# Mixture of experts on one core: one compact iteration per expert, and fp32 products without splits for experts of at most 64 tokens

## The chip, the cores and the metric

The kernel runs on one core of a Trainium2 chip. The metric is the device time of one execution in microseconds (us). The kernel before was timed three times; the median counts.

## The reference

One decoder block for 512 tokens of width 1024. The first half (state-space mixer, pooling mixer, gates) is not touched by the change. The second half sends every token to 8 of 64 experts:

```python
_, top_e = lax.top_k(masked, TOP_K)                # 512 tokens x 8 experts
def expert_block(args):                            # 128 slots of one expert
    toks, ws, e = args
    xb = u_pad[toks]
    hid = jax.nn.silu(xb @ we_gate[e]) * (xb @ we_up[e])    # 1024 -> 256, twice
    return (hid @ we_down[e]) * ws[:, None]                 # 256 -> 1024
```

All is float32. Each expert has three weights of 1 MB (gate, up, down). The routing of these inputs is uneven: 34 experts have at most 64 tokens (two of them none; expert 0, with 49, is one of the 34), 19 have 65 to 128, and 11 have 132 to 165. In the order 0 to 63, with l for at most 64, h for 65 to 128, H for more and 0 for none:

```
lhHHllHlHllHhl0hlhllHHlhHllhHlHlhhhhllllhhlll0hhlllhhllHhhlllllh
```

## The kernel before

TensorE (PE) multiplies fp32 numbers as three fp32r products. `split` (lines 43 to 46) makes a high part on ACT (a cast) and a low part on DVE (a subtraction), and `mm3` (lines 58 to 62) issues high by high, low by high and high by low. Both operands are split: the tokens (`turn`: gathered rows are transposed on PE, 8 transposes of 128x128, and evacuated as `xh` and `xl`) and the weights (`Unit.split`: 128x2048 from a raw tile into `h` and `l`, three of them per expert).

`experts` holds the 64 experts as straight-line code, one iteration for each, with the instructions written out by hand (`manual_schedule`). Tokens sit in blocks of 128 slots: a block of an expert is gathered from DRAM by GpSimd (`gather`, an indirect DMA into `xg`), multiplied, weighted and added to the output rows by another indirect DMA (`scatter`). An expert of more than 128 tokens has a second block. The text says single for an iteration of one block and double for one of two.

In iteration e of a single, PE multiplies gate and up of expert e (`gate_up_mm`, 8 slices of the contraction, 24 instructions of 512 columns), transposes the tokens of e+1, multiplies down of e-1 (`down`, 12 instructions of 512 columns), transposes the hidden rows of e (`down_in`), and makes the slot list of e+4 (`index`, tile `ixp`). Beside it ACT and DVE split gate and up of e+1 and down of e. One branch at the head of the iteration chooses between the code for one block, for none and for two:

```python
with tc.If(n_e <= P) as big:            # line 1113
    with tc.If(n_e > 0) as some:        # line 1114
        ...
with big.Else():
    turn(k, k.xg[3 + e % 2], xnext)
```

SP loads the weights (`load(e + 2)` in iteration e; a load is skipped for an expert without tokens) into eight raw tiles of 1 MB that are used in turn, so a tile is written again eight units, or 2.67 experts, later. It is free once the split that reads it is done. GpSimd's queue holds the gathers and scatters, each within conditionals by the number of rows; line 1065 is the conditional of the second block.

Of the kernel before, what the change touches and what calls it, by code (L numbers as in the profile page):

```python
# [21 lines left out]
P = 128  # L22
T = 512
NT = 4
D = 1024
NK = 8
H = 32
G = 8
E = 64
NC = 8  # L30
# [814 lines left out]

def slot_onehot(k, pm, nb, eng):

    oh = k.wp.tile([P, NT, nb, P], BF16, name="oh", bufs=2)
    for t in range(NT):
        eng.tensor_scalar(oh[:, t], k.iota[:, :nb, :], pm[:, t:t + 1], None, op0=ALU.is_equal)  # L850
    return oh
# [21 lines left out]
    return xg  # L873


def turn(k, src, x, full=None):

    nc = k.nc
    xv = src.rearrange("p (q k) -> p k q", k=NK)
    for hf in range(2):  # L880
        ps = k.xt.tile([P, 512], F32, name="xt", tag="xt")
        for q in range(4):
            nc.tensor.transpose(ps[:, q * P:(q + 1) * P], xv[:, hf * 4 + q, :], k.ident)  # L883
        ks = slice(hf * 4, hf * 4 + 4)
        pv = ps.rearrange("p (q t) -> p q t", q=4)
# [4 lines left out]
    return x  # L890


def split_pair(hp, lp):
# [46 lines left out]
    return ps  # L940


def gate_act(k, ps):
    nc = k.nc
    hid = k.wp.tile([P, 256], F32, name="hid", bufs=2)
# [5 lines left out]
def down_in(k, hid, hx):  # L951
    nc = k.nc
    hv = hid.rearrange("p (q j) -> p j q", j=2)
    ps = k.ht.tile([P, 2, P], F32, name="ht", tag="ht")
    for j in range(2):
        nc.tensor.transpose(ps[:, j, :], hv[:, j, :], k.ident)
    nc.scalar.copy(hx[0], ps)  # L957
    nc.vector.tensor_sub(hx[1], ps, hx[0].bitcast(F32))  # L958
    return hx


# [52 lines left out]
def experts(k, shared):  # L1014
    nc, tc, a = k.nc, k.tc, k.a
    ET = mybir.EngineType
    idx, xg, gu, dn, oh, counts = {}, {}, {}, {}, {}, {}
# [17 lines left out]
    def onehot(e):  # L1035
        if e < E:
            oh[e] = slot_onehot(k, k.posm[:, :, e], 2, nc.vector)
# [48 lines left out]
    gu[0][0].split(k, k.gu0w[0])  # L1086
    gu[0][1].split(k, k.gu1w)
    shared()
    onehot(4)
    load(1)  # L1090
    dn[0].split(k, k.dnw[0])
    turn(k, xg[0], k.xT[0])
    with tc.manual_schedule():
        fetch_over(0)
        fetch_over(1)
        for e in range(E):
            more = e + 1 < E
            xT, xnext = k.xT[e % 2], k.xT[(e + 1) % 2]
            hx, hlast = k.hx[e % 2], k.hx[(e + 1) % 2]
            fetch(e + 2)  # L1100

            def last_down(n):
                if e > 0:
                    down(k, hlast, dn[e - 1], n, k.yl[(e + 1) % 2], idx[e - 1][1][:, 0:1])

            def splits():
                if more:
                    gu[e + 1][0].split(k, k.gu0w[(e + 1) % 2])
                if e > 0:
                    dn[e].split(k, k.dnw[e % 2])  # L1110

            n_e = count(e, (ET.PE, ET.Activation, ET.DVE))
            with tc.If(n_e <= P) as big:
                with tc.If(n_e > 0) as some:
                    g0 = gate_up_mm(k, xT, gu[e])
                    splits()
                    hid = gate_act(k, g0)
                    if more:
                        turn(k, xg[e + 1], xnext)
                        gu[e + 1][1].split(k, k.gu1w)  # L1120
                    last_down(0)
                    last_down(1)
                    down_in(k, hid, hx)
                with some.Else():
                    splits()
                    if more:
                        turn(k, xg[e + 1], xnext)
                        gu[e + 1][1].split(k, k.gu1w)
                    last_down(0)
                    last_down(1)  # L1130
            with big.Else():
                turn(k, k.xg[3 + e % 2], xnext)
                g0 = gate_up_mm(k, xT, gu[e])
                splits()
                hid = gate_act(k, g0)
                g1 = gate_up_mm(k, xnext, gu[e])
                hid1 = gate_act(k, g1)
                down_in(k, hid, hx)
                if more:
                    turn(k, xg[e + 1], xnext)  # L1140
                last_down(0)
                down_in(k, hid1, k.hx[2])
                last_down(1)
                if more:
                    gu[e + 1][1].split(k, k.gu1w)
                for n in range(2):
                    down(k, k.hx[2], dn[e], n, k.xg[2], idx[e][1][:, 1:2])
            fetch_over(e + 2)
            onehot(e + 5)
# [6 lines left out]
        for n in range(2):  # L1156
            down(k, k.hx[e % 2], dn[e], n, k.yl[e % 2], idx[e][1][:, 0:1])
# [80 lines left out]
def block_kernel(ctx, tc, a, out):  # L1238
    nc = tc.nc
    k = Ctx()  # L1240
# [52 lines left out]
    with ExitStack() as p2:  # L1293
        raw2 = p2.enter_context(tc.tile_pool(name="raw2", bufs=2))
        k.wp = p2.enter_context(tc.tile_pool(name="wp", bufs=1))
        k.raws += [raw2.tile([P, 2048], F32, name="raw", tag="raw") for _ in range(2)]
        k.yl = [k.zp.tile([P, D], F32, name="yl", tag="zs") for _ in range(2)]
        k.hx = [tuple(k.wp.tile([P, 2, P], F32R, name=f"h{n}{i}") for n in "hl") for i in range(3)]
        spx = ExitStack()
        sp = spx.enter_context(tc.tile_pool(name="sp", bufs=1))  # L1300
# [45 lines left out]
```

## Time and profile before

| what | value |
|---|---|
| three runs | 1673.65, 1677.66, 1679.98 us (median 1677.66) |
| profiled execution | 1690.4 us, of which 1688.7 us span |
| PE, DVE, ACT, POOL busy | 90%, 76%, 54%, 26% of the span |
| expert stage (first iteration to last scatter) | 805 to 1645 us |
| mean granted clock of PE | 0.959 of full speed |

The profile follows one execution. Its parts give each engine's busy time, the span in 40 slices, the DMA queues, the chain of work that ended last and the costliest groups of instructions. A matmul's shown duration includes its way through the array, so the cost of one among many is read from start to start. An fp32 product (not fp32r) appears as two matmul instructions.

### The profile page before, as it was taken

Reading aid. Unit: us, or ns where it says so; the run is one execution under the profiler, and the core shown is the slowest. Engines: PE = TensorE matmul, PEld = TensorE weight load, DVE = VectorE, ACT = ScalarE, POOL = GpSimd, SP = SyncE. Lnnn points to the kernel's source line nnn. Section 1 sums busy time; section 2 is a strip of 40 time slices with the busy share of each in tenths; the row PEclk is TensorE's granted clock in tenths of the full one; section 3 lists DMA queues with packets and bytes.
Section 4 is the critical chain, followed back from the end, with each engine's and each line's share of the span. In section 5 each row is a group of like instructions: output and inputs, shape, how many; then the busy total and the mean of one; then the engine's idle time right before and its main releaser. Section 6 shows DMA issues by size and latency. Waiting matters only on the chain.

```text
span 1688.7 us, 23424 instructions
## 1 busy us (share of the span) xinstructions
PE 1527.1 (90%) x7900; PEld 1267.4 (75%) x7900; DVE 1280.2 (76%) x1938; ACT 919.2 (54%) x1122; POOL 440.5 (26%) x312
## 2 busy tenths in 40 slices
PE   5999999999999999999898988898899988989980
PEld 5888788787888778887687776787677876777760
DVE  6888878778787974558666769776669889985856
ACT  3555545345343223335565657676567777775752
POOL 5211101002010110320233334332324233441426
PEclk7999999999999999999899999999999999999995
DMA  9442433333342345235967759868879988996954
GB/s 289 116 125 84 142 100 111 101 97 109 95 131 88 107 134 197 88 130 208 356 186 273 245 158 347 308 216 254 278 240 312 350 287 292 314 313 232 326 168 153
DMA packets 152118, 340.26 MB, mean 201 GB/s; under 512 B 15816, under 2 KB 94832, under 8 KB 142272
## 3 DMA queue, kind: packets, MB, share of 16 engines
q1 hardware_dynamic: 135888, 294.94, 51.8%
q0 software_dynamic: 15408, 40.23, 9.3%
q8 instruction: 120, 1.97, 0.5%
q10 hardware_dynamic: 576, 2.10, 0.3%
q14 instruction: 126, 1.03, 0.2%
HBM read 314.00 MB, written 31.01 MB: 204 GB/s over the span
## 4 chain that ended last, share of the span: by engine, by line
PE 53%; DMA 21%; issue 10%; DVE 9%; POOL 3%; ACT 3%; POOLq 0%; another core or an unknown queue 0%; SPq 0%; DVEq 0%; ACTq 0%
PE mm L62 8%; PE mm L60 8%; PE mm L61 8%; DMA xg<-u2d,idx 8%; DMA raw<-in_we_up_dram 5%; PE gu L60 4%; PE gu L62 4%; PE gu L61 4%; DMA Y<-xg,idx 4%; DVE wl L45 2%; DMA Y<-yl,idx 2%; PE xt L883 2%; PE sd L476 1%; PE yo L60 1%; PE yo L62 1%
## 5 line engine op out<-in xcount | busy, mean ns | idle before, releaser
L45 DVE TENSOR_TENSOR wl<-raw,wh 128x2048 fp32r<-128x2048 f32 x180 | 422.0, 2358 | 96.8 <-ACT wh L44 86.2
L44 ACT CAST wh<-raw 128x2048 fp32r<-128x2048 f32 x180 | 341.2, 1918 | 88.2 <-PE mm L61 64.2
L983 POOL DMA_INDIRECT Y<-yl,idx x64 | 132.5, 2070 | 482.6 <-ACT hh L957 238.5
L60 PE MATMUL gu<-wh,xh 128*128 128x512 f32 x444 | 184.0, 414 | 8.6 <-issue 6.6
L62 PE MATMUL gu<-wh,xl 128*128 128x512 f32 x444 | 180.3, 406 | 2.1 <-issue 2.1
L61 PE MATMUL gu<-wl,xh 128*128 128x512 f32 x444 | 180.5, 407 | 0.4 <-DVE hl L958 0.4
L60 PE MATMUL mm<-uh,wh 128*128 128x512 f32 x432 | 171.2, 396 | 1.9 <-ACT zs L284 1.9
L62 PE MATMUL mm<-uh,wl 128*128 128x512 f32 x432 | 169.8, 393 | 0.0
L61 PE MATMUL mm<-ul,wh 128*128 128x512 f32 x432 | 169.0, 391 | 0.0
L45 DVE TENSOR_TENSOR pair<-raw,pair 128x2048 fp32r<-128x2048 f32 x66 | 148.5, 2289 | 25.2 <-ACT pair L44 18.4
L871 POOL DMA_INDIRECT xg<-u2d,idx x75 | 126.0, 1680 | 97.6 <-DVE oh L850 27.5
L946 ACT ACTIVATE hid<-gu 128x256 f32<-128x256 f32 x73 | 28.1, 385 | 203.6 <-PE gu L62 203.6
L44 ACT CAST pair<-raw 128x2048 fp32r<-128x2048 f32 x66 | 123.2, 1923 | 15.8 <-DMA raw<-in_ws_up_dram 12.4
L883 PE MATMUL xt<-ident,xg 128*128 128x128 f32 x632 | 89.8, 286 | 36.7 <-issue 20.3
L883 PEld LDWEIGHTS xt<-ident,xg 128*128 128x128 f32 x632 | 84.0, 194 | 43.6 <-issue 36.2
L889 DVE TENSOR_TENSOR xl<-xt,xh 128x512 fp32r<-128x512 f32 x150 | 96.9, 685 | 20.3 <-ACT xh L888 18.8
L60 PEld LDWEIGHTS gu<-wh,xh 128*128 128x128 f32 x444 | 87.9, 198 | 27.5 <-issue 8.1
L888 ACT CAST xh<-xt 128x512 fp32r<-128x512 f32 x150 | 81.5, 590 | 45.2 <-PE xt L883 42.1
L61 PEld LDWEIGHTS gu<-wl,xh 128*128 128x128 f32 x444 | 87.6, 197 | 23.6 <-issue 3.9
L62 PEld LDWEIGHTS gu<-wh,xl 128*128 128x128 f32 x444 | 87.2, 196 | 20.5
L60 PEld LDWEIGHTS mm<-uh,wh 128*128 128x128 f32 x432 | 81.2, 188 | 20.2 <-ACT zs L284 2.3
L947 DVE TENSOR_TENSOR hid<-hid,gu 128x256 f32<-128x256 f32 x73 | 30.4, 417 | 85.7 <-ACT hid L946 85.7
(341 smaller groups left out, 3568.7 us busy)
## 6 DMA issues: line engine op xcount, KB each, us to landing
raw<-in_we_gate_dram SPq DMA_DIRECT2D x124, 512.0 KB
raw<-in_we_up_dram SPq DMA_DIRECT2D x124, 512.0 KB
raw<-in_we_down_dram SPq DMA_DIRECT2D x62, 1024.0 KB
raw<-in_w_in_dram SPq DMA_DIRECT2D x27, 1024.0 KB
raw<-in_w_ada_dram SPq DMA_DIRECT2D x16, 1024.0 KB
big<-in_w_ada_dram SPq DMA_DIRECT2D x16, 512.0 KB
raw<-in_w_in_dram SPq DMA_DIRECT2D x16, 512.0 KB
raw<-in_w_br_ssd_dram SPq DMA_DIRECT2D x8, 1024.0 KB
```

Of the source, the lines that this page charges most:

```text
L44: nc.scalar.copy(h, raw)
L45: nc.vector.tensor_sub(l, raw, h.bitcast(F32))
L60: nc.tensor.matmul(out, sh, mh, start=first, stop=False)
L61: nc.tensor.matmul(out, sh, ml, start=False, stop=False)
L62: nc.tensor.matmul(out, sl, mh, start=False, stop=last)
L871: k.nc.gpsimd.indirect_dma_start(out=xg[:n], out_offset=None, in_=k.u2d, bounds_check=T - 1, oob_is_err=False, in_offset=bass.IndirectOffs ...
L883: nc.tensor.transpose(ps[:, q * P:(q + 1) * P], xv[:, hf * 4 + q, :], k.ident)
L888: nc.scalar.copy(x[0][:, ks, :], pv)
L889: nc.vector.tensor_sub(x[1][:, ks, :], pv, x[0][:, ks, :].bitcast(F32))
L946: nc.scalar.activation(hid, ps[:, :256], AF.Silu)
L947: nc.vector.tensor_mul(hid, hid, ps[:, 256:])
L983: k.nc.gpsimd.indirect_dma_start(out=k.Y[acc], out_offset=bass.IndirectOffsetOnAxis(ap=idx[0][:n, b:b + 1], axis=0), in_=y[:n], in_offset= ...
```

## The change

1. Every iteration is now one sequence for all experts. What depends on the count stands in short conditional pieces of its own: `by_count` (at most 64 tokens, or more), `if_two` (a second block) and `if_heavy` (more than 64). An iteration has five of them on PE and eight each on ACT and DVE.
2. For an expert of at most 64 tokens (not expert 0) the weights are not split. `gate_up_light` multiplies the raw weights as fp32, 64 slots by 256 columns, the gate into PSUM partitions 0 to 63 and the up half into partitions 64 to 127 of the same bank. `down_light` does the same with the two halves of the output columns. Silu and the product of the two halves come after the transpose, on 128x128 instead of 128x256.
3. An expert without tokens takes the same path with what its buffers hold; nothing of it is scattered.
4. The transposes of a second block move from the head of its own iteration to the iteration before.
5. The one-hot tile has one buffer instead of two, and is made at the head of the iteration for e+4 (before: at its end for e+5).
6. The light pieces read the raw tiles on PE, so SP's loads wait for PE's semaphore as well: a tile is free after the gate and up product of its expert, or after its down product, where before it was free after the split.

```diff
+LIGHT = 64
-    oh = k.wp.tile([P, NT, nb, P], BF16, name="oh", bufs=2)
+    oh = k.wp.tile([P, NT, nb, P], BF16, name="oh")
...
+def gate_up_light(k, x, units, ps):
+    for kk in range(NK):
+        w = units[kk // 4].raw.rearrange("p (s k f) -> p s k f", k=4, s=2)
+        for s in range(2):
+            nc.tensor.matmul(ps[s * LIGHT:(s + 1) * LIGHT, :256], x[:, kk, :], w[:, s, kk % 4, :], start=kk == 0, stop=kk == NK - 1)
+
+def down_light(k, x, unit, y, w):
+    ps = k.yo.tile([P, 512], F32, name="yo", tag="yo")
+    for j in range(2):
+        for n in range(2):
+            nc.tensor.matmul(ps[n * LIGHT:(n + 1) * LIGHT, :], x[:, j, :], unit.raw[:, j * D + n * 512:j * D + n * 512 + 512],
+                             start=j == 0, stop=j == 1)
+    for n in range(2):
+        nc.scalar.activation(y[:LIGHT, n * 512:(n + 1) * 512], ps[n * LIGHT:(n + 1) * LIGHT, :], AF.Copy, scale=w[:LIGHT])
...
+    def by_count(e, engines, light, heavy):
+        if e == 0:
+            heavy()
+        elif e < E:
+            with tc.If(count(e, engines) <= LIGHT) as small:
+                light()
+            with small.Else():
+                heavy()
+    def if_two(e, engines, body):
+        if e < E:
+            with tc.If(count(e, engines) > P):
+                body()
...
+    def products(e):
+        def light():
+            gate_up_light(k, k.xf, gu[e], g)
+            nc.scalar.copy(hid, g[:, :256])
+        def heavy():
+            gate_up_mm(k, k.xT[e % 2], gu[e], g)
+            if e > 0:
+                dn[e].split(k, k.dnw[e % 2])
+            gate_act(k, g, hid)
+        by_count(e, every, light, heavy)
+    def turned(e):
+        halves = turn_in(k, xg[e])
+        def light():
+            for hf, pv in enumerate(halves):
+                nc.scalar.copy(k.xf[:, hf * 4:hf * 4 + 4, :], pv[:, :, :LIGHT])
+        def heavy():
+            turn_out(k, halves, k.xT[e % 2])
+            gu[e][1].split(k, k.gu1w)
+        by_count(e, both, light, heavy)
+    def turned_over(e):
+        if_two(e, every, lambda: turn(k, k.xg[3 + e % 2], k.xT[(e + 1) % 2]))
...
         for e in range(E):
...
+            if_heavy(e + 1, both, lambda: gu[e + 1][0].split(k, k.gu0w[(e + 1) % 2]))
+            hid = products(e)
+            hid1 = hidden(k)
+            if_two(e, every, lambda: gate_act(k, gate_up_mm(k, k.xT[(e + 1) % 2], gu[e]), hid1))
+            turned(e + 1)
+            turned_over(e + 1)
+            downs(e - 1)
+            hidden_turned(e, hid)
+            def second_down():
                 down_in(k, hid1, k.hx[2])
                 for n in range(2):
                     down(k, k.hx[2], dn[e], n, k.xg[2], idx[e][1][:, 1:2])
+            if_two(e, every, second_down)
```

The order of PE's instructions at the head of an iteration of the kernel before: two branches, then the three-product code.

```order
L1055 UNCONDITIONAL_BRANCH
L1113 COMPARE_AND_BRANCH
L1114 COMPARE_AND_BRANCH
L60 MATMUL gu<-wh,xh_6486 128x512
L61 MATMUL gu<-wl,xh_6486 128x512
L62 MATMUL gu<-wh,xl_6487 128x512
```

The same place now. The 16 fp32 products of the light piece come first (`raw` is the unsplit weight, `xf` the unsplit tokens); a branch jumps over the other piece.

```order
L1158 UNCONDITIONAL_BRANCH
L1146 COMPARE_AND_BRANCH
L962 MATMUL gu<-raw,xf 64x256 x16
L1146 UNCONDITIONAL_BRANCH
L61 MATMUL gu<-wh,xh_6488 128x512
L62 MATMUL gu<-wl,xh_6488 128x512
L63 MATMUL gu<-wh,xl_6489 128x512
```

Where before the 24 products of 512 columns followed directly, an execution now runs one of two pieces of 16 or 24.

PE further on in the iteration, with the semaphores that each row waits for: the transposes of a second block, if there is one, and then the down product of the expert before.

```order
L885 MATMUL xt<-ident,xg_5335 128x128 [waits DVE_49,PE_49,Activation_49]
L885 MATMUL xt<-ident,xg_5335 128x128 x3
L1153 UNCONDITIONAL_BRANCH
L1153 UNCONDITIONAL_BRANCH [waits PE_49]
L1146 COMPARE_AND_BRANCH
L971 MATMUL yo<-raw,hT 64x512 [waits DMAHW3_49,DMAHW1_49,DMAHW5_49,DVE_49,DMAHW6_49,Activation_49]
```

The row that waits for `PE_49`, PE's own semaphore, is the path of an expert without a second block: PE waits there until all it has issued is done, adds what the skipped piece would have added to the semaphore, and goes on. An iteration has three such places on PE (lines 1153 three times), and ACT and DVE have them too. Before, no iteration of PE had one.

## Rows read from the trace of the kernel before

**Rows 1.** The page's parts 1 and 2: whole span, 40 equal slices.
```profile
PE 1527.1 (90%) x7900; PEld 1267.4 (75%) x7900; DVE 1280.2 (76%) x1938; ACT 919.2 (54%) x1122; POOL 440.5 (26%) x312
...
PE   5999999999999999999898988898899988989980
...
PEclk7999999999999999999899999999999999999995
DMA  9442433333342345235967759868879988996954
```

**Rows 2.** Stretches: expert stage, one single, two double blocks, a run of singles.
```profile
core 0: us, PE busy (x) PEld busy (x) DVE busy (x) ACT busy (x) POOL busy (x), PEclk, DMA share, GB/s
805.00:1645.00 840.00, 756.10 (x3890) 624.26 (x3890) 639.66 (x910) 561.55 (x638) 285.39 (x148) 0.95 0.82 273
1127.50:1137.30 9.80, 9.80 (x56) 8.26 (x55) 9.63 (x16) 8.38 (x10) 6.04 (x4) 1.00 0.97 260
1148.20:1172.90 24.70, 23.97 (x114) 19.71 (x115) 12.23 (x20) 13.75 (x17) 3.08 (x2) 0.93 0.70 234
1108.20:1127.50 19.30, 19.30 (x98) 15.80 (x97) 11.96 (x19) 11.37 (x15) 5.93 (x4) 1.00 0.59 199
1275.40:1361.00 85.60, 80.48 (x435) 66.80 (x434) 78.21 (x114) 66.61 (x73) 29.70 (x17) 0.98 1.02 344
```

**Rows 3.** The page's part 5: splits, and the gate's Silu, one per block.
```profile
L45 DVE TENSOR_TENSOR wl<-raw,wh 128x2048 fp32r<-128x2048 f32 x180 | 422.0, 2358 | 96.8 <-ACT wh L44 86.2
L44 ACT CAST wh<-raw 128x2048 fp32r<-128x2048 f32 x180 | 341.2, 1918 | 88.2 <-PE mm L61 64.2
...
L946 ACT ACTIVATE hid<-gu 128x256 f32<-128x256 f32 x73 | 28.1, 385 | 203.6 <-PE gu L62 203.6
```

**Rows 4.** Timeline of PE: a single block's iteration (start us, us).
```profile
1129.91 1.05 PE L883 MATMUL xt<-ident,xg 128*128 128x128 f32 x8
1130.72 0.48 PE L60 MATMUL yo<-wh,hh 128*128 128x512 f32 x1
1131.03 0.39 PE L61 MATMUL yo<-wl,hh 128*128 128x512 f32 x1
...
1133.56 0.39 PE L956 MATMUL ht<-ident,hid 128*128 128x128 f32 x2
1133.79 0.34 PE L860 MATMUL ixp<-V,oh 128*128 128x5 bf16 x8
1133.99 0.48 PE L60 MATMUL gu<-pair,xh 128*128 128x512 f32 x1
1134.31 0.39 PE L61 MATMUL gu<-pair,xh 128*128 128x512 f32 x1
1134.54 0.39 PE L62 MATMUL gu<-pair,xl 128*128 128x512 f32 x1
1134.77 0.40 PE L60 MATMUL gu<-pair,xh 128*128 128x512 f32 x1
```

**Rows 5.** Timeline of PE: an fp32 product of 256 columns (line 458).
```profile
169.78 0.59 PE L458 MATMUL sd<-xdec,Bt 128*128 128x256 f32 x2
170.03 0.58 PE L60 MATMUL mm<-yTh,wh 128*128 128x512 f32 x1
170.44 0.39 PE L61 MATMUL mm<-yTl,wh 128*128 128x512 f32 x1
```

**Rows 6.** Timeline of PE: four fp32 products of 128 columns (line 434).
```profile
144.61 1.05 PE L434 MATMUL tr<-CT,BT 128*128 128x128 f32 x8
145.42 0.48 PE L62 MATMUL mm<-uh,wl 128*128 128x512 f32 x1
```

**Rows 7.** DMA queues in the expert stage, 805 to 1645 us.
```profile
q1 hardware_dynamic: 44176, 192.96, 65.0%
q0 software_dynamic: 12220, 32.92, 16.1%
```

**Rows 8.** PE's branches at line 1114: count, ns min/median/max.
```profile
L1114 PEldq COMPARE_BRANCH  x106: 67/188/6792, 808.1 to 1637.2; - x106
```

**Rows 9.** POOL's waits where a conditional is skipped, line 1065.
```profile
L1065 POOLq INC_SWDGE_SEM  x106: 817/1594/2685, 795.8 to 1640.4; - x106
```

**Rows 10.** Timeline of PE: entering a double block.
```profile
1144.90 0.35 PE L860 MATMUL ixp<-V,oh 128*128 128x5 bf16 x8
1148.93 1.13 PE L883 MATMUL xt<-ident,xg 128*128 128x128 f32 x8 [3.68 <-DMA Y<-yl,idx]
```

More of the change, by code (lines that the diff above doesn't have):

```diff
@@ L873, in gather, with turn_in @@
     return xg
-def turn(k, src, x, full=None):
+def turn_in(k, src):
     nc = k.nc
     xv = src.rearrange("p (q k) -> p k q", k=NK)
+    halves = []
     for hf in range(2):
@@ L883, in turn, with turn_out @@
             nc.tensor.transpose(ps[:, q * P:(q + 1) * P], xv[:, hf * 4 + q, :], k.ident)
+        halves.append(ps.rearrange("p (q t) -> p q t", q=4))
+    return halves
+def turn_out(k, halves, x, full=None):
+    nc = k.nc
+    for hf, pv in enumerate(halves):
         ks = slice(hf * 4, hf * 4 + 4)
-        pv = ps.rearrange("p (q t) -> p q t", q=4)
         if full is not None:
@@ L890, in turn @@
     return x
+def turn(k, src, x, full=None):
+    return turn_out(k, turn_in(k, src), x, full)
 def split_pair(hp, lp):
@@ L940, in gate_up_mm, with hidden, gate_act @@
     return ps
-def gate_act(k, ps):
+def gate_up_light(k, x, units, ps):
     nc = k.nc
-    hid = k.wp.tile([P, 256], F32, name="hid", bufs=2)
+    for kk in range(NK):
[3 more added lines that the diff above has]
+def down_light(k, x, unit, y, w):
+    nc = k.nc
+    ps = k.yo.tile([P, 512], F32, name="yo", tag="yo")
[5 more added lines that the diff above has]
+        nc.scalar.activation(y[:LIGHT, n * 512:(n + 1) * 512], ps[n * LIGHT:(n + 1) * LIGHT, :], AF.Copy, scale=w[:LIGHT])
+def hidden(k):
+    return k.wp.tile([P, 256], F32, name="hid", bufs=2)
+def gate_act(k, ps, hid=None):
+    nc = k.nc
+    hid = hidden(k) if hid is None else hid
     nc.scalar.activation(hid, ps[:, :256], AF.Silu)
@@ L1088, in experts @@
     shared()
-    onehot(4)
     load(1)
@@ L1092, in experts, with if_heavy, downs, heavy @@
     turn(k, xg[0], k.xT[0])
+    every, both = (ET.PE, ET.Activation, ET.DVE), (ET.Activation, ET.DVE)
+    def by_count(e, engines, light, heavy):
[10 more added lines that the diff above has]
+                body()
+    def if_heavy(e, engines, body):
+        if e < E:
+            with tc.If(count(e, engines) > LIGHT):
+                body()
+    def products(e):
+        g, hid = k.gu.tile([P, 512], F32, name="gu", tag="gu"), hidden(k)
+        def light():
[7 more added lines that the diff above has]
+        by_count(e, every, light, heavy)
+        return hid
+    def turned(e):
+        if e == E:
+            return
+        halves = turn_in(k, xg[e])
+        def light():
+            for hf, pv in enumerate(halves):
+                nc.scalar.copy(k.xf[:, hf * 4:hf * 4 + 4, :], pv[:, :, :LIGHT])
[5 more added lines that the diff above has]
+        if_two(e, every, lambda: turn(k, k.xg[3 + e % 2], k.xT[(e + 1) % 2]))
+    def downs(e):
+        if e < 0:
+            return
+        y, w = k.yl[e % 2], idx[e][1][:, 0:1]
+        def heavy():
+            for n in range(2):
+                down(k, k.hx[e % 2], dn[e], n, y, w)
+        by_count(e, every, lambda: down_light(k, k.hT, dn[e], y, w), heavy)
+    def hidden_turned(e, hid):
+        ps = hidden_in(k, hid)
+        def light():
+            nc.scalar.activation(k.hT, ps[:, :, :LIGHT], AF.Silu)
+            nc.vector.tensor_mul(k.hT, k.hT, ps[:, :, LIGHT:])
+        by_count(e, both, light, lambda: hidden_out(k, ps, k.hx[e % 2]))
     with tc.manual_schedule():
@@ L1095, in experts @@
         fetch_over(1)
+        turned_over(0)
         for e in range(E):
-            more = e + 1 < E
-            xT, xnext = k.xT[e % 2], k.xT[(e + 1) % 2]
-            hx, hlast = k.hx[e % 2], k.hx[(e + 1) % 2]
             fetch(e + 2)
[L1102 to L1141, printed above, removed]
+            fetch_over(e + 2)
+            onehot(e + 4)
+            for i in (e, e + 1):
+                if i < E:
+                    for engines in (every, both):
+                        count(i, engines)
@@ L1155, in experts @@
         e = E - 1
-        for n in range(2):
-            down(k, k.hx[e % 2], dn[e], n, k.yl[e % 2], idx[e][1][:, 0:1])
+        downs(e)
         first(e, lambda n: scatter(k, idx[e], 0, k.yl[e % 2], 1, n))
```

17 lines of the change are left out of this document (9 added, 8 removed).

## The prediction

> **What bounds the kernel now.** I read the page first: the change touches only the stage of the experts, so I look for where that stage begins and what is full in it. PE is busy for nearly all of every slice, at full clock, but the DMA row rises from 2 to 5 tenths to 5 to 9 in the second half of the span [rows 1]. The table of stretches then shows the expert stage, 840 of the 1688.7 us, with PE busy for 756 us, DVE 640, ACT 562 and the DMA engines for 82% [rows 2]. Three resources are near their limit there, and which one decides differs from iteration to iteration.
>
> A single (one block of 128 slots) takes 9.8 us when nothing disturbs it, with PE busy for all of it and DVE for 9.63 [rows 2]. PE's timeline adds up to that: 36 products of 512 columns start 0.23 us apart, 5.5 for gate and up and 2.8 for down, then 0.81 for eight transposes and 0.2 each for the hidden transposes and the slot list [rows 4]. DVE's 9.6 are mostly three splits of 2.36 us, with three casts of 1.92 on ACT beside them [rows 3]. So singles have PE and DVE level, and cutting one alone would give little.
>
> A double takes 24.7 us when entered from a single and 19.3 from another double [rows 2]. The difference is at its head: PE stands for 3.68 us after the far branch [rows 10]. The letters show nine of the eleven doubles entered from a single or none and two from a double, so doubles take 9 × 24.7 + 2 × 19.3 = 261 us, a mean of 23.7. The other 579 us of the stage belong to 53 singles: 10.9 each, not 9.8. The run of singles from 1275 to 1361 us says why: the DMA engines are full (share 1.02) at 344 GB/s [rows 2].
>
> The transfers of an expert can be priced. The weight queue took 65.0% of 840 us, 546 us, for 192.96 MB [rows 7]; at 3.146 MB an expert that is 61.3 experts, 8.9 us each. Gathers and scatters took 16.1%, 135 us [rows 7]. By rows moved (rounded up to 16) a fifth of it, 26 us, belongs to the 33 light experts (at most 64 tokens, without expert 0), 0.8 each; 58 us to the other 20 singles, 2.9 each; 50 us to the doubles. So a light expert needs 9.7 us of DMA time and another single 11.8, whatever PE does. Two light experts load nothing.
>
> **The change, part by part.**
>
> (a) *Light experts on PE.* An fp32 product of 256 columns costs 0.43 us: from 169.78 to 170.44 less the 0.23 of the fp32r product in between [rows 5, 4]. Four of 128 columns take 0.81 [rows 6], 0.20 each, so the cost grows with the columns and 512 take 0.86. Gate and up are 16 × 0.43 = 6.9 us, down 4 × 0.86 = 3.4: 10.3 in sum if one product runs after the other, against 8.3 for the three-product code. If the two halves run side by side it is 5.2. No row of this trace has two products in different halves of the columns, so these are my two bounds. I take 5.2: two neighbouring products write different partitions and none waits for the other, and PE does overlap what doesn't collide: its weight loads are busy for 75% of the span and its matmuls for 90% of the same span [rows 1], so most loads run beside a matmul.
>
> The Trainium skill, TensorEngine Tiling (Array Packing), section "Key Properties", says that column tiles work independently, while a change of tiling mode drains the engine. No run here shows either yet; with the first rule the sum stands as below, and without it it would be rival A's.
>
> With transposes, hidden transposes and slot list (1.2 us) a light iteration is 6.4 us on PE before its branches.
>
> (b) *Skipped pieces.* An iteration without a second block passes three places where PE must finish all it has issued. The trace before has no such place on PE. Below, the cost is nothing if the branch and the wait hide behind work. Above, the nearest rows are GpSimd's skips at 1.59 us in the median [rows 9]; PE's own branches take 0.07 to 0.19 us, though one took 6.8 [rows 8]. I take 0.5 us each: about 0.16 for the end of the last matmul (0.39 shown against a spacing of 0.23 [rows 4]), 0.2 for the branch and some 0.15 to refill. That is nearer PE's own row. So 1.5 us in each of the 53 singles: light 7.9 us, others 9.8 + 1.5 = 11.3.
>
> (c) *Light iterations in sum.* PE needs 7.9 us, DVE has lost its splits, but DMA needs 9.7. So DMA decides: 9.6 in the mean with the two empty ones, against 10.9 now. 33 × 1.3 = **43 us gained**. What PE gains beyond that only waits for transfers.
>
> (d) *Singles over 64 tokens.* 11.3 by PE, 11.8 by DMA, part of which doubles absorb: 11.5 against 10.9. 20 × 0.6 = **12 us lost**.
>
> (e) *Doubles.* 48 products of gate and up (11.0 us), 24 of down (5.5), two sets of transposes (1.6, one of them now in the iteration before), hidden transposes and slot list (0.7): 18.8 us. The far branch goes. A new wait comes in: the second block's hidden transposes are followed at once by its down product, with only cast and subtraction between, some 2.2 us that the other down product covered before. 21.0 against 23.7: 11 × 2.7 = **30 us gained**.
>
> (f) *Waits on ACT and DVE.* They pass eight conditionals where they passed two, and a raw tile is freed up to an iteration later because PE now reads it, so loads start later and can pile up behind each other on SP's queue. Cover for a late load is 2.67 experts of tiles. I bound it by 0 and 1.5 us an iteration (eight branches at PE's 0.19 [rows 8]) and take 0.4, nearer the lower end because most of them stand beside a split of 2 us: 64 × 0.4 = **26 us lost**. The one-hot tile with one buffer costs nothing: DVE already waits for the slot list at the end of each iteration.
>
> Sum: −43 + 12 − 30 + 26 = −35. The profiled execution took 1690.4 us, so 1655; the median of the runs stands at 1677.66 / 1690.4 = 0.9925 of it, so **1643 us**.
>
> **Rivals.**
>
> A. *The halves run one after the other.* A light iteration is 10.3 + 1.2 + 1.5 = 13.0 us on PE instead of 9.6 or 10.9. (c) becomes 33 × 2.1 = +70, the sum +78, the time 1768 × 0.9925 = 1755: slower. Against it speaks that nothing in the code orders the halves; for it, that no row shows it. It decides as soon as running together saves less than about a quarter: the sum is zero where 33 × (p + 2.7 − 10.9) = −8, so at p = 8.0 of the 10.3.
>
> B. *Skips cost more.* At 1.2 us each, light iterations go to 10.0 (PE), other singles to 13.4: −30 + 50 − 30 + 26 = +16, 1706 × 0.9925 = 1693. It decides from about 1.1 us a skip. For it: the 1.59 of GpSimd and the 3.68 at a far branch; against it: PE's usual 0.07 to 0.19.
>
> C. *Nothing is lost at the conditionals.* Singles stay with their DMA time (light −43, others 0), doubles fall to 19.3 (−48): −91, 1599 × 0.9925 = 1587. This is near a floor, since the DMA engines are busy for 82% of 840 = 690 us.
>
> D. *The light path isn't taken often enough.* The Silu row counts 73 blocks with the four of the shared expert apart [rows 3]: 62 experts with tokens and 11 second blocks, as the routing says. So 33 it is, and I give D no chance.
>
> **How the numbers follow.** Forecast, 1612 to 1668: 0.45. C, 1580 to 1612: 0.08. B, 1668 to 1735: 0.17. A, 1715 to 1790: 0.30. A measurement of this kernel can tell about 0.5%, 8 us, from no change. Faster than 1669: all of C and nearly all of the forecast, 0.52. Within 1669 to 1686: the lower third of B and a remnant, 0.09. Slower: the rest of B and all of A, 0.39. The range of 8 in 10 is 1600 to 1755: half of C, all of the forecast and of B, half of A. The forecast's own range is 1612 to 1668.
>
> **What would show it.** Two products at line 962 that start together, or about 0.11 us apart for each matmul instruction, say that (a) holds; 0.21 or more says A. Light iterations of about 9.6 us with a DMA share near 1 and PE waiting for raw tiles would confirm (c); light iterations of 13 with DMA below 0.8, A. Gaps of PE after line 962 and after the transposes give (b) directly. A double entered from a single at 21 us, without 3.7 us of standing at its head, confirms (e). I would be wrong if PE were the bound of light iterations, or if singles over 64 tokens went above 12.5 us.

## The result, and the profile after

The changed kernel takes **1725.9 us** (median of 4 runs, 1721.0 to 1730.9) against 1678.8 for the kernel before on the same chips: ratio 1.029, interval 1.025 to 1.032, **slower by 47 us**. I had forecast 1643. The time lies in the range given, on its wrong side.

The page of the changed kernel, first lines and parts 1, 2 and 5 (columns as in [rows 1] and [rows 3]):

```profile
span 1719.3 us, 26061 instructions
PE 1497.8 (87%) x8084; PEld 1181.8 (69%) x8084; DVE 1013.1 (59%) x1744; ACT 747.2 (43%) x1027; POOL 368.6 (21%) x312
...
PE   6999999999999999999788888788788888887870
...
PEclk9999999999999999999999999899998999998995
DMA  9343433333242263255576859768868999997874
...
L46 DVE TENSOR_TENSOR wl<-raw,wh 128x2048 fp32r<-128x2048 f32 x114 | 273.2, 2401 | 96.9 <-ACT wh L45 82.3
...
L962 PE MATMUL gu<-raw,xf 128*64 128x256 f32 x1056 | 123.7, 381 | 6.8 <-DMA raw<-in_we_down_dram 1.8
```

The light path is taken by all 33 experts (1056 = 33 × 32 records), DVE is 267 us and ACT 172 us less busy, and PE 29 us. Every engine does less and the kernel takes longer. The table of stretches for the stage of the experts, against [rows 2]:

```profile
core 0: us, PE busy (x) PEld busy (x) DVE busy (x) ACT busy (x) POOL busy (x), PEclk, DMA share, GB/s
...
805.00:1645.00 840.00, 701.58 (x3993) 520.99 (x3993) 366.16 (x717) 377.01 (x526) 209.13 (x145) 0.95 0.80 265
```

PE falls from 756 to 702 us, and the DMA share from 0.82 to 0.80 (in the same 840 us; the changed kernel's stage goes on to 1676): over the whole stage nothing has taken PE's place as the bound. Something stands in between. To see where, I cut the stage into iterations, each ending with the slot-list instruction on DVE, and sorted them by the expert and the one after it (L light or empty, S one block over 64 tokens, D double). Mean us of an iteration, in the profiled executions:

| this, next | count | before | changed | all heavy | copies, own PSUM |
|---|---|---|---|---|---|
| L, L | 16 | 10.4 | 9.5 | 11.3 | 9.2 |
| L, S | 8 | 10.1 | 12.0 | 11.5 | 10.9 |
| L, D | 6 | 10.8 | 15.0 | 14.0 | 11.8 |
| S, L | 8 | 11.3 | 10.2 | 11.3 | 10.3 |
| S, S | 7 | 11.3 | 12.4 | 11.2 | 11.5 |
| S, D | 3 | 12.1 | 16.4 | 13.2 | 14.7 |
| D, any | 11 | 23.7 | 22.7 | 22.6 | 20.4 |

(The last two columns are experiments, below.) A light expert followed by a light one takes the time that I forecast, 9.5, though not for the reason that I gave (see the account of (c) below). What is lost stands in front of heavy experts: 38 us in the nine singles before a double alone, 23 in L, S and S, S. With one stretch per iteration, the DMA share of the light ones falls from 0.97 to 0.88, that of the other singles from 0.93 to 0.81.

One such place, expert 27 between a light one and a double. ACT's and PE's timelines in the changed kernel:

```profile
1217.03 0.28 ACT L1212 ACTIVATE hT<-ht 128x128 f32<-128x128 f32 x1
1223.62 3.70 ACT L45 CAST wh<-raw 128x2048 fp32r<-128x2048 f32 x2 [6.32 <-DMA raw<-in_we_gate_dram]
1227.23 0.38 ACT L984 ACTIVATE hid<-gu 128x256 f32<-128x256 f32 x1
1227.95 1.07 ACT L897 CAST xh<-xt 128x512 fp32r<-128x512 f32 x2 [0.34 <-DVE wl L46]
```

```profile
1222.88 1.13 PE L885 MATMUL xt<-ident,xg 128*128 128x128 f32 x8 [0.51 <-DMA xg<-u2d,idx]
1231.62 1.94 PE L885 MATMUL xt<-ident,xg 128*128 128x128 f32 x8 [7.62 <-DVE xl L898]
```

At the head of iteration 27 ACT is to cast a tile of expert 28, and stands 6.3 us for its landing. Everything of expert 27 queues behind it on ACT, and PE stands 7.6 us until its PSUM tiles of transposes are evicted. SP's timeline says why the tile is late:

```profile
1206.42 0.33 SPq L932 DMA_DIRECT2D raw<-in_we_gate_dram  x1
...
1209.11 0.33 SPq L932 DMA_DIRECT2D raw<-in_we_gate_dram  x1
1209.55 0.47 SPq L933 DMA_DIRECT2D raw<-in_we_up_dram  x1
```

The last two rows are its loads. They went out eight us before ACT was ready for the tile at 1217.3, and the tile was there 14 us after their issue. The first row is a load of expert 27: SP had stood 11.7 us ahead of it, for PE's down product of expert 24, and two tiles of expert 27 went out first. The DMA engines were full (share 0.99 from 1208.7 to 1219.2).

SP's waits in the stage of the experts (line, released by, us in total, times, longest), first of the kernel before, then of the changed one:

```profile
SPq L919 <- DVE xl L889: 311.7, 54, 16.6
SPq L919 <- DMA raw<-in_we_gate_dram: 102.7, 67, 7.5
```

```profile
SPq L932 <- PE yo L61: 295.8, 28, 25.6
SPq L932 <- PE yo L971: 179.7, 29, 15.6
```

Loads waited for DVE, which frees a raw tile when it has split it, an iteration ahead of the products (the row names DVE's subtraction of the tokens, which stands between two splits). Now they wait for PE's down products, of light (L971) and of heavy experts (L61) alike. From the issue of an expert's first gate load to the start of its iteration there were 39.8 us in the mean (experts 4 to 59), at least 29.6; now 29.4, and 13 of them are under 22, down to 16.6.

### The profile page after: what moved, and what is told of

It is laid out like the page before. It is cut to its first block, busy times and chain, and to the rows that moved or that the text cites. A ratio compares the mean times of both kernels' runs of the same rounds, so it can differ in the third digit from the quotient of the medians.

```text
span 1719.3 us, 26061 instructions
## 1 busy us (share of the span) xinstructions
PE 1497.8 (87%) x8084; PEld 1181.8 (69%) x8084; DVE 1013.1 (59%) x1744; ACT 747.2 (43%) x1027; POOL 368.6 (21%) x312
## 5 line engine op out<-in xcount | busy, mean ns | idle before, releaser
L46 DVE TENSOR_TENSOR wl<-raw,wh 128x2048 fp32r<-128x2048 f32 x114 | 273.2, 2401 | 96.9 <-ACT wh L45 82.3
L45 ACT CAST wh<-raw 128x2048 fp32r<-128x2048 f32 x114 | 216.7, 1907 | 132.0 <-PE mm L62 65.6
L61 PE MATMUL mm<-uh,wh 128*128 128x512 f32 x432 | 171.9, 398 | 1.9 <-ACT zs L285 1.9
L962 PE MATMUL gu<-raw,xf 128*64 128x256 f32 x1056 | 123.7, 381 | 6.8 <-DMA raw<-in_we_down_dram 1.8
L962 PEld LDWEIGHTS gu<-raw,xf 128*64 128x64 f32 x1056 | 99.0, 137 | 19.2 <-issue 3.6
L61 PE MATMUL gu<-wh,xh 128*128 128x512 f32 x256 | 103.2, 403 | 3.0 <-PE ixp L861 1.1
L62 PE MATMUL gu<-wl,xh 128*128 128x512 f32 x256 | 101.9, 398 | 0.2 <-DVEq L1153 0.2
L63 PE MATMUL gu<-wh,xl 128*128 128x512 f32 x256 | 101.4, 396 | 0.0
L46 DVE TENSOR_TENSOR pair<-raw,pair 128x2048 fp32r<-128x2048 f32 x33 | 75.0, 2290 | 43.8 <-ACT pair L45 32.4
L61 PEld LDWEIGHTS mm<-uh,wh 128*128 128x128 f32 x432 | 81.6, 189 | 20.3 <-ACT zs L285 2.3
L63 PEld LDWEIGHTS mm<-uh,wl 128*128 128x128 f32 x432 | 81.5, 189 | 17.6 <-issue 0.9
L62 PEld LDWEIGHTS mm<-ul,wh 128*128 128x128 f32 x432 | 81.7, 189 | 16.9 <-issue 0.4
L971 PE MATMUL yo<-raw,hT 128*64 128x512 f32 x264 | 73.0, 677 | 17.6 <-ACTq L1153 5.5
```

Source lines behind the costliest of these rows:

```text
L45: nc.scalar.copy(h, raw)
L46: nc.vector.tensor_sub(l, raw, h.bitcast(F32))
L61: nc.tensor.matmul(out, sh, mh, start=first, stop=False)
L62: nc.tensor.matmul(out, sh, ml, start=False, stop=False)
L63: nc.tensor.matmul(out, sl, mh, start=False, stop=last)
L962: nc.tensor.matmul(ps[s * LIGHT:(s + 1) * LIGHT, :256], x[:, kk, :], w[:, s, kk % 4, :], start=kk == 0, stop=kk == NK - 1)
```

## The experiments

All ratios are to the kernel before. They differ from the quotients of the medians by up to 0.5%, some 8 us, so a difference between two runs that is smaller than this shows little.

| run | us | ratio, interval |
|---|---|---|
| all_heavy | 1733.9 | 1.035 (1.031 to 1.040) |
| empty_arm | 1750.6 | 1.045 (1.040 to 1.050) |
| light_unused | 1777.4 | 1.060 (1.054 to 1.065) |
| before_6_tiles | 1681.2 | 1.002 (1.000 to 1.005) |
| before_5_tiles | 1703.7 | 1.016 (1.013 to 1.018) |
| gate_then_up | 1777.5 | 1.058 (1.053 to 1.062) |
| light_reads_copy | 1665.4 | 0.992 (0.989 to 0.994) |
| late_split | 1721.8 | 1.026 (1.022 to 1.030) |
| copy_and_late | 1676.9 | 0.998 (0.996 to 1.000) |
| copy_own_psum | 1642.0 | 0.979 (0.977 to 0.981) |
| own_psum | 1707.0 | 1.013 (1.009 to 1.018) |
| heavy_own_psum | 1717.9 | 1.023 (1.018 to 1.028) |
| heavy_one_more_piece | 1750.5 | 1.041 (1.036 to 1.046) |
| copy_merged_2 | 1686.2 | 1.004 (1.002 to 1.006) |

**1. The frame without light work.** Three kernels build the change up: the compact iteration with every expert heavy, then the branches, then the light code in them, used by the two empty experts alone.

```diff
 # all_heavy, in by_count and if_heavy
-            with tc.If(count(e, engines) <= LIGHT) as small:
-                light()
-            with small.Else():
-                heavy()
+            heavy()
-            with tc.If(count(e, engines) > LIGHT):
-                body()
+            body()
 # empty_arm: with tc.If(count(e, engines) > 0): heavy()
 # light_unused: the change, with 0 for LIGHT in the two conditions
```

Expected of all_heavy:

> The compact iteration alone: every expert takes the three-product path, and only the pieces of the second block stay conditional, so PE never reads a raw tile. Theory L (raw tiles come free later because PE reads them, so loads start later and the DMA engines idle): gate loads start some 38 to 40 us ahead of their expert again (before 39.8, changed kernel 29.4), singles keep their DMA time, and the time is near the kernel before, 1665 to 1695. Theory S (the conditionals themselves cost it): two skipped pieces a single stay, so 1700 to 1715. Theory H (the change between light and heavy work, with PE standing and at half clock, costs it): no such change is left, 1670 to 1690.

Expected of empty_arm:

> As the changed kernel, with every conditional piece on every engine, but the arm of the light path is empty and is taken by the two empty experts alone; PE reads no raw tile. Theory L: loads start as early as in the run with all experts heavy, and the time is 10 to 20 us above it for the added branches, 1680 to 1710. Theory S: all the conditionals are there, so about as slow as the changed kernel, 1715 to 1740. Theory H: 1675 to 1695.

Expected of light_unused:

> As the changed kernel, with the limit of the light path at 0 tokens instead of 64: the code of the light path is there, but only the two empty experts take it. SP's loads must still wait for PE's part on both paths. Theory L: loads start about 10 us later than with the empty arm although nothing light is computed, and the time is 20 to 50 us above it, 1715 to 1750. Theory S: the same as with the empty arm. Theory H: no light work, so near the kernel before, 1675 to 1695.

Measured: +56, then +17, then +27 us; and from there to the changed kernel −51, which is what light products give. So the light path earns its share, and the frame around it costs 99. Theory H falls (nothing light is left in these runs), theory L too as the only cause: all_heavy loads 44.0 us ahead and is 56 us slower. That is also more than theory S gave it (1715 at most, and 1740 for empty_arm), so the frame costs more than I expected of conditionals. L shows in the third step, in SP's waits of empty_arm and then of light_unused:

```profile
SPq L932 <- DVE wl L46: 394.0, 79, 15.0
```

```profile
SPq L932 <- PE yo L61: 553.5, 52, 25.7
```

Though PE reads no heavy expert's raw tile, SP waits for it: the load's wait is fixed in the program and must hold for either arm. The lead falls from 45.6 to 32.2 us, and ACT's standing for weights rises from 17 to 49. Part of the 27 us is also branches: PE's gaps at the two two-armed pieces grow by some 0.4 us an iteration, in 53 singles up to 21 us. This step alone doesn't separate the two.

**2. Is it the lead?** The kernel before with fewer raw tiles (four fresh ones become two, then one).

Expected of before_6_tiles:

> The kernel before with six raw tiles instead of eight, so one expert's loads less far ahead, and no conditional, product or split changed. Theory L: this takes some 8 to 10 us from the lead of the loads and so costs about what the change cost, 1705 to 1745. Theories S and H: the lead of the loads matters little, 1678 to 1690.

Expected of before_5_tiles:

> The kernel before with five raw tiles. Six cost nothing although loads then started 30 us ahead as in the changed kernel; but there the shortest lead of a gate load was 22.7 us, and in the changed kernel leads of 16 to 20 us stand in front of its worst iterations. Theory L (it is the short leads that cost, once a load no longer lands before the cast one iteration ahead): with five tiles leads fall to 15 to 22 us, ACT waits for landing weights by more than 60 us, 1710 to 1780. If the lead is of no account and the copies helped for another reason: again 1675 to 1690.

Six tiles cost nothing clear of the noise (3 us), though the mean lead falls to 30.2, as in the changed kernel. That spoke against L as I had put it. But no lead was under 22.7 there. With five the mean is 27.7, eleven are under 22, and 27 us are lost, somewhat less than expected. ACT's waits in the five-tile run, then in the changed kernel:

```profile
ACT wh L44 <- DMA raw<-in_we_up_dram: 40.0, 17, 6.8
ACT pair L44 <- DMA raw<-in_we_up_dram: 34.5, 14, 5.8
```

```profile
ACT wh L45 <- DMA raw<-in_we_up_dram: 18.2, 10, 5.1
ACT pair L45 <- DMA raw<-in_we_up_dram: 17.7, 4, 8.3
ACT wh L45 <- DMA raw<-in_we_gate_dram: 17.6, 5, 6.3
ACT pair L45 <- DMA raw<-in_we_gate_dram: 10.3, 7, 4.7
```

So it isn't the mean lead that costs. Nor is it the lead to an expert's own iteration: ten of the 13 leads under 22 us in the changed kernel belong to light experts, for which nothing is cast ahead, and expert 28 of the example has 29.6. What fits is the time from the issue of the first gate load to the head of the iteration before, where the first cast of a heavy expert stands. In the kernel before it is at least 19.1 us, with six tiles 12.8. With five, 18 of 26 heavy experts have less than that, down to 10.7. In the changed kernel eleven have less, down to 7.4, and at four of its five largest losses (the iterations ahead of experts 51, 20, 28 and 55) it is 8.4, 8.5, 10.1 and 10.1. With the copies of the next experiment it is at least 19.0.

**3. The light path with its tiles freed early.**

```diff
+    def copy(self, k, pair):
+        self.h, self.l = pair
+        k.nc.scalar.copy(self.h, self.raw)
-        w = units[kk // 4].raw.rearrange("p (s k f) -> p s k f", k=4, s=2)
+        w = units[kk // 4].h.bitcast(F32).rearrange("p (s k f) -> p s k f", k=4, s=2)
```

and `copy` in the light arms where the heavy ones split; the light down product reads `unit.h` too.

Expected of light_reads_copy:

> As the changed kernel, but a light expert's three raw tiles are copied by ACT (1.9 us each, where the other path casts) into the buffers of the split weights, and its products read those; so PE reads no raw tile and SP's loads wait for ACT and DVE alone. The light products take the weights as the cast to fp32r leaves them, so that part is computed with rounded weights. Theory L (late loads: ACT, DVE and PE waited 90 us for landing weights in the changed kernel, 14 in the kernel before): gate loads start about 40 us ahead again, these waits fall below 25 us, light iterations before a heavy one lose 2 us or more, and the time is 1680 to 1705. Theory S (conditionals and PE's order alone): waits may shrink, but the time stays at 1720 to 1740, the copies adding to ACT.

Expected of late_split:

> As the changed kernel, but the split of the second gate-up unit comes after the transposes of a second block instead of between the two sets of transposes (one conditional more on ACT and DVE in each iteration). Theory P (the second set of transposes stands because its PSUM tiles are freed by ACT and DVE behind that cast; 37 us of PE in front of 11 doubles): the wait between the two sets falls from 3.4 us to about 2 a double and the time by 10 to 25, to 1700 to 1716. Rival: those waits come from late weights or from fetching the code of the second block, and the time stays at 1720 to 1740.

Expected of copy_and_late:

> Both edits together: light products from copies (with the weights rounded by the cast, as in the run with the copy alone) and the later split. If the two losses are separate, the gains add: with theories L and P 1665 to 1690; with S alone 1715 to 1740.

The copies give **60 us** back, more than expected, though ACT works 175 us more: 1665, now below the kernel before. The lead is 41.9, and ACT's largest waits for weights are these:

```profile
ACT wh L45 <- DMA raw<-in_we_up_dram: 3.4, 3, 1.6
ACT wh L927 <- DMA raw<-in_we_up_dram: 3.0, 6, 1.5
```

The DMA share of the light iterations is back at 0.91, of the other singles at 0.93. Theory P is a miss: the later split gains 4 us, which is within the noise (the wait between the two sets of transposes only goes from 3.4 to 3.1 a double), and with copies it costs 11. Of the 37 us that PE stood there, 17 went with the copies: they were late weights.

**4. Do the two halves run side by side?** In gate_then_up the loops are swapped: all gate products (lower half), then all up products.

```diff
-    for kk in range(NK):
-        w = units[kk // 4].raw.rearrange("p (s k f) -> p s k f", k=4, s=2)
-        for s in range(2):
+    for s in range(2):
+        for kk in range(NK):
+            w = units[kk // 4].raw.rearrange("p (s k f) -> p s k f", k=4, s=2)
```

Expected of gate_then_up:

> As the changed kernel, but a light expert's gate products (lower half of the partitions) all come before its up products (upper half), and likewise the two halves of its down product, so that neighbouring products share a half. If two products run beside each other only when neighbours lie in different halves, each matmul instruction of gate and up takes about 0.21 us instead of 0.108 and a light expert 5.2 us more on PE: light iterations of 11 to 14 us, time 1735 to 1850. If the halves don't matter (each 64-column product is simply that short), the spacing stays at 0.108 and the time at 1720 to 1732.

PE's timeline: a light iteration between light ones in the changed kernel (expert 43) with the head of the next, then gate and up of one light expert in gate_then_up (start us, us):

```profile
1428.53 3.76 PE L962 MATMUL gu<-raw,xf 128*64 128x256 f32 x32 [0.24 <-ACTq L1153]
1432.60 1.13 PE L885 MATMUL xt<-ident,xg 128*128 128x128 f32 x8 [0.30 <-PEq L1153]
1434.37 1.94 PE L971 MATMUL yo<-raw,hT 128*64 128x512 f32 x8 [0.64 <-ACTq L1153]
1436.24 0.51 PE L994 MATMUL ht<-ident,hid 128*128 128x128 f32 x2
1436.90 0.34 PE L861 MATMUL ixp<-V,oh 128*128 128x5 bf16 x8
1437.49 3.77 PE L962 MATMUL gu<-raw,xf 128*64 128x256 f32 x32 [0.26 <-PE ixp L861]
```

```profile
1473.26 6.29 PE L962 MATMUL gu<-raw,xf 128*64 128x256 f32 x32 [0.15 <-ACT yl L1026]
```

The time shown for the products of line 962 includes 0.38 us of the last record. In the change, records start 0.108 us apart in the mean (0.090 and 0.126 in turn): 32 take 3.5 us. With the halves in sequence they start 0.216 apart; only where the last gate products meet the first up products are there pairs. So a product next to one of the other half runs beside it, and next to one of its own half it waits. Light iterations between light ones go from 9.5 to 12.1 us. The Trainium skill, TensorE: Matmul & The Clock Gate, section "Step-by-step: what each phase is for", says that matmuls stay in program order. Up to the seam, where up follows gate, the run agrees: twelve gate records start alone, 0.216 us apart, though the up products need nothing of them. At the seam it differs: by the profile's starts the first three up records (1475.87, 1476.14, 1476.36) come before the last gate record (1476.52, the one that raises the semaphore), with the same spacing in all 33 light experts.

**5. The doubles' standstill.** The second block's hidden transposes needed the one PSUM tile `ht` that the first block's had just filled.

```diff
-                down_in(k, hid1, k.hx[2])
+                xt = k.xt.tile([P, 512], F32, name="xt", tag="xt")
+                hidden_out(k, hidden_in(k, hid1, xt[:, :256].rearrange("p (j t) -> p j t", j=2)), k.hx[2])
```

Expected of copy_own_psum:

> As the run with light products from copies (weights rounded by the cast there), and the hidden transposes of a second block go into a PSUM tile of the input transposes instead of waiting for the one that the first block's have just filled (2.0 us of PE in each of 11 doubles). If that wait is for the PSUM tile: it falls to about 1 us, 5 to 12 us gained, 1653 to 1662. If it is the product's wait for cast and subtraction of the hidden values that counts, it only moves behind the transposes: 1662 to 1668.

Expected of own_psum:

> The changed kernel with the second block's hidden transposes in a PSUM tile of their own, and the light products from the raw tiles as in the change. If the losses by late loads and by this wait are separate, the same 20 to 25 us are gained, 1700 to 1708. If PE's standstill in the doubles only gave the loads time that they now need: 1712 to 1726.

Expected of heavy_own_psum:

> The run with all experts heavy, and the second block's hidden transposes in a PSUM tile of their own. With copies this took the standstill of PE out of the doubles (from 1.95 us each to about 0.5) and the slow clock behind it, and gave 23 us. If that loss belongs to the compact iteration: 1708 to 1718 here (all heavy had 1734), doubles at about 20.4 us. If it was bound up with the light path: 1728 to 1738.

−23, −19 and −16 us by the medians (−21, −26 and −21 by the ratios): the loss is there with and without light work, and adds to that of the loads. With copies it is twice what I expected and more. In heavy_own_psum the doubles take 21.6 us, not the 20.4 that I expected: PE still stands 2.2 us in nine of them, for 1.7 of that until DVE is through a split and past the skipped piece behind it. PE's timeline of expert 24, with copies alone, and then with a PSUM tile of its own:

```profile
1179.24 0.39 PE L998 MATMUL ht<-ident,hid 128*128 128x128 f32 x2
1180.99 0.47 PE L998 MATMUL ht<-ident,hid 128*128 128x128 f32 x2 [1.36 <-DVE hl L1005]
1181.97 0.79 PE L61 MATMUL yo<-pair,hh 128*128 128x512 f32 x1 [0.51 <-ACT hh L1004]
1182.57 0.63 PE L62 MATMUL yo<-pair,hh 128*128 128x512 f32 x1
1182.99 0.63 PE L63 MATMUL yo<-pair,hl 128*128 128x512 f32 x1
...
1185.41 0.39 PE L63 MATMUL yo<-pair,hl 128*128 128x512 f32 x1
```

```profile
1159.01 0.39 PE L999 MATMUL ht<-ident,hid 128*128 128x128 f32 x2
1159.24 0.40 PE L999 MATMUL xt<-ident,hid 128*128 128x128 f32 x2
1160.49 0.51 PE L61 MATMUL yo<-pair,hh 128*128 128x512 f32 x1 [0.85 <-ACT hh L1005]
1160.83 0.40 PE L62 MATMUL yo<-pair,hh 128*128 128x512 f32 x1
1161.07 0.44 PE L63 MATMUL yo<-pair,hl 128*128 128x512 f32 x1
```

Behind the standstill the next products start 0.43 us apart instead of 0.23. The table of stretches gives the granted clock for those 4.4 us, and for the same products in the other run:

```profile
1181.00:1185.40 4.40, 3.89 (x10) 3.00 (x11) 0.42 (x1) 0.79 (x2) 0.99 (x1) 0.61 0.99 224
```

```profile
1160.40:1163.40 3.00, 2.91 (x12) 2.10 (x12) 0.55 (x2) 0.73 (x2) 1.36 (x1) 1.00 1.03 253
```

0.61 and 1.00: most of the first stretch ran at 1.2 GHz. Nine of the eleven doubles have it in one run (a mean spacing over 0.34 in the twelve products behind, against 0.24), three in the other; in the changed kernel eight have it. The length of the standstill alone does not decide: in the changed kernel experts 3 and 24 both stand 1.36 and 0.51 us, and the products behind start 0.24 us apart at expert 3 and 0.38 at expert 24. What does decide stays open.

**6. The price of a skipped piece.**

```diff
+            if_two(e, every, lambda: down_in(k, hid1, k.hx[2]))
             def second_down():
-                down_in(k, hid1, k.hx[2])
```

Expected of heavy_one_more_piece:

> The run with all experts heavy, with the last conditional piece of an iteration (the second block's hidden transposes and its down product) cut into two conditional pieces one behind the other; no work is added or moved. Theory S (a skipped piece costs each single 0.3 to 0.5 us): 53 skips more and 11 taken, 1748 to 1765. If what the compact iteration costs lies in the doubles alone: 1732 to 1740.

One more piece costs 17 us by the medians, 14 by the profiled spans, 10 by the ratios. PE's timeline where it is passed, in all_heavy and here:

```profile
1374.97 0.39 PE L994 MATMUL ht<-ident,hid 128*128 128x128 f32 x2
1375.51 0.34 PE L861 MATMUL ixp<-V,oh 128*128 128x5 bf16 x8
```

```profile
1401.04 0.39 PE L994 MATMUL ht<-ident,hid 128*128 128x128 f32 x2
1401.99 0.35 PE L861 MATMUL ixp<-V,oh 128*128 128x5 bf16 x8 [0.57 <-PEq L1150]
```

0.54 becomes 0.95, and over 39 singles the iteration is 0.39 us longer. Three such pieces in 53 singles are some 60 us, of which a part hides where loads are the bound.

**7. One piece fewer, a miss.** The second block's transposes were moved into the piece of its gate and up products, first without and then with the gather moved behind them.

Expected of copy_merged:

> As the run before it, and the transposes of a second block stand in front of its gate and up products, in the same conditional piece: one skipped piece fewer in each iteration, no transposes of a second block at the end of the iteration ahead (20 us of PE in front of the doubles), but their casts are now waited for in the double. Theory S (a skipped piece costs every single 0.3 to 0.5 us, 53 of them): 10 to 25 us gained, and 11 times some 2 us lost in the doubles; in sum 1640 to 1665. If skipped pieces cost nothing: 1665 to 1685.

Expected of heavy_merged:

> The run with all experts heavy, with the transposes of a second block moved into the piece of its gate and up products: one skipped piece fewer in each iteration. Theory S: 53 times 0.3 to 0.5 us gained, and 16 us in front of the doubles against some 25 us in them: 1705 to 1730 (all heavy had 1734). If skipped pieces cost nothing and the doubles' own order does: 1735 to 1755.

Expected of copy_merged_2:

> The run with copies and own PSUM tile (light weights rounded by the cast), with the second block's transposes in front of its gate and up products in the same conditional piece, and the gather of the second block after next behind that piece, so that its tile is free. One skipped piece fewer in each iteration, and the 20 us of PE in front of the doubles gone; against it some 2 to 3 us in each double, where casts and subtractions of the second block are waited for, and the slow clock after it. Theory S: 1620 to 1640. If skipped pieces are nearly free and the doubles' waits decide: 1642 to 1665.

In the first two (1709.9 and 1841.1) the gather for a later expert comes ahead of the transposes and writes the same tile, so second blocks are computed on other rows and the transposes wait for that gather: their times say nothing on the question. In the third the gather is in its place, and it is 44 us slower than copy_own_psum, not up to 22 faster. One row of its waits tells why:

```profile
PE xt L885 <- DVEq L1158: 75.1, 37, 4.1
```

The piece now holds evictions of the two `xt` tiles. In 37 iterations the next expert's transposes wait 2 us for DVE, not to evict anything but to come past the skipped piece, which stands behind the multiplication of the hidden values in DVE's program. It is SP's wait for PE over again, on other engines.

## Why the prediction was wrong

**What failed first is step (f).** I put all waits of ACT, DVE and SP at 0.4 us an iteration, 26 us, "nearer the lower end" of 0 to 1.5. The late loads alone are 60 us (light_reads_copy), 0.9 an iteration; the branches of light and heavy add 17 (empty_arm). Both ends held, the choice did not. I had written that loads start later and can pile up, and then let 2.67 experts of tiles cover it. That is true of the mean: six tiles cost nothing. It isn't where a heavy expert, whose first cast comes an iteration ahead, finds tiles that the code now holds until PE has come past their products.

**Second is step (e).** I wrote that doubles gain 30 us. Doubles and the iterations before them lost 28 in the profiled execution. The wait ahead of the second down product was sized well, 2.2 us against 1.9 measured, but nothing was put down for the slow clock behind it: twelve products some 0.15 us further apart in eight of eleven doubles, 14 us in all (nine and 16 with copies). The 3.68 us at the head [rows 10] went, as forecast; in its place PE stands 3.4 us between the two sets of transposes at the end of the iteration before, which no term held. With both causes taken away, doubles and their forerunners are 22 us shorter than before: (e) would have come near.

(a) was right to the tenth: 3.5 and 1.7 us, 5.2 in sum, against 10.3 had the halves followed each other. Rival A, at 0.30, falls; gate_then_up shows that its mechanism is real and hangs on the order of two loops. The Trainium skill's rule from TensorEngine Tiling (Array Packing), "Key Properties", held for neighbours in different halves, at 0.108 us a record.

(b) took 0.5 us for a skipped piece; 0.4 measured. Rival B needed 1.1 and falls. But (b) counted three of PE's five pieces and put the two with two arms at nothing. In the iteration of expert 43 shown above, PE needs 8.96 us from head to head; 6.4 are work, as (a) had it, and the other 2.5 stand about the pieces, where (b) had 1.5.

(c) came out only where a light expert is followed by a light one, 9.5 us, and there by luck. It said that DMA decides, with PE waiting for raw tiles. In these 16 iterations the DMA share is 0.91, and PE waits 1.1 us in all for raw tiles. Its own sequence fills the time: from head to head 8.9 to 9.1 us behind a light expert (9.8 at expert 38), and 9.4 to 9.9 behind a heavy one, whose down product is longer. So PE was the bound of these iterations, one of the two signs of being wrong that I had named. Its base was off as well: 10.9 was the mean of all singles, and light ones took 10.4 before, the others 11.4. (d) gave 11.5 for the other singles; they take 12.1, 10.2 before a light one and 16.4 before a double.

The forecast was 83 us too low: some 50 in (f) (77 for 26), and, the late loads counted there, some 35 in (e) (with copies, doubles and forerunners still lay 6 us over the kernel before, where I had 30 under). The two profiled executions differ by 30.6 us only, because that of before lay 12 us above its median and that of the change 5 below. No run separates the three frame costs of the compact iteration to the microsecond: of its 56 us, the standstill in the doubles is 16 to 21; three skipped pieces at 0.4 us are the largest part by estimate, since no run takes all three away; the rest stays open.

The best version, copy_own_psum, takes 1642 us, 2.1% less than the kernel before, with light weights rounded by the cast. It has the DMA share at 0.92 in all singles, doubles at 20.4 us, and is, by chance, where I had forecast the change itself to be.

## What to carry to other kernels

When an engine begins to read a buffer that another used to free, ask how far ahead of its first reader the next load starts at the worst pair of neighbours, not in the mean. A conditional piece that is skipped keeps its waits: whoever waits for a buffer used in either arm waits until each engine has come past it. Price a standstill of PE with the slow clock that can follow it.

## What the hardware showed unexpectedly

A standstill of 1.4 and 0.5 us with two transposes between, 2 us together, was followed by 4.4 us at a granted clock of 0.61; one of 0.85 us at the same place was not. Yet the same 1.36 and 0.51 us at expert 3 of the changed kernel were followed by products at full pace. Two fp32 products into different halves of the partitions run side by side as neighbours in the program, at 0.108 us a record against 0.216. With one half behind the other, they do so only at the seam, where the first three up records start before the last gate record.
